# Moving a statistics visit and 98 adds between engines in a hybrid decoder kernel whose order a planner writes

## The chip, the cores and the metric

The kernel runs on one core of a Trainium2 chip. The metric is the device time of one execution in microseconds. An order of instructions is fixed for each of five queues: TensorE (PE), VectorE (DVE), ScalarE (ACT), GpSimd (POOL), and SyncE (SP), which here issues all DMAs.

## The reference

One decoder layer over 4096 tokens of width 1024, in float32: a root-mean-square norm, one input projection, two groups of heads that read it, a gate on each, one output projection, a residual add and a final norm.

```
h = rmsnorm(x, norm_w);  u = h @ w_in
GLA, 4 heads:   S_t = diag(a_t) S_{t-1} + k_t^T v_t;  o_t = q_t S_t    (in chunks)
                o = o * rsqrt(mean(o^2) + eps) * gla_norm_w;  gla_out = o * silu(gg)
RWKV, 8 heads:  mixed = cols + (prev - cols) * mu;  r, rk, rv, wl, al = split(mixed)
                kk = rk * k_k / |rk * k_k|        (norm over the head's 64 columns)
                k  = rk * (1 + (a - 1) * k_a)
                S_t = S_{t-1} (diag(w_t) - kk_t^T (a_t kk_t)) + v_t^T k_t;  y_t = S_t r_t
                y  = group_norm(y) * ln_w + ln_b
                bonus = sum(r * k * r_k over the head) * v
                rwkv_out = (y + bonus) * silu(rg)
out = rmsnorm(x + concat(gla_out, rwkv_out) @ w_out, final_norm_w)
```

## The kernel before, in words

Activations are held with the features on the partitions and 512 tokens along the free dimension: 8 blocks of 512 tokens. In each block the RWKV group is worked off in 4 units of two heads (128 partitions), 32 units in all, and the GLA group in 2 pairs. Every large projection is made of fp16 parts: 8 matmuls for each of three products of high and low halves, 24 of 128x128 by 128x512. The weights are split into these halves in the first block, from raw tiles that SP loads 512 KB at a time, and stored to DRAM, from where later blocks load them again.

A sum over the features of a head, or of all partitions, is a *statistics visit* (`stat_mm`, L816): four float32 matmuls with a 128x32 matrix of ones and zeros, each writing 32 rows of one PSUM bank, so the array works as four tiles of 128x32. The profile shows each float32 matmul as two, so a visit is eight. In `rwkv_ab` (L961) a unit has two: the key norm (`stat_mm(pst, bones, rn)`, L995), whose result goes through a reciprocal root (`newton`) and over DRAM to all partitions (`bcast`, one store and two broadcasting loads), and, near the unit's end, the bonus sum (L1063), which is copied by ScalarE, spread in the same way and multiplied by v on VectorE. `rwkv_d` (L1183) has the third, of the output norm, and adds the bonus to it. `bones` has ones in column 0 for the first head and in column 16 for the second, so two of every 32 result rows are used.

The squares of the input (`x_block`, L867) and of the output (`out_block`, L1382) are summed over 8 feature tiles before one visit: ScalarE squares a tile, GpSimd adds it. GpSimd also runs most units' 62-step triangular inversion on small tiles.

The program text does not fix the order. Eight streams (input blocks, weights, the RWKV chain, its inverse, GLA, the two projections and the output) generate steps with their dependences. A planner then runs a list schedule forwards and backwards over all steps with costs of its own (`cost`, `forward`, `backward`), 24 rounds of it (`ROUNDS`; a nonzero seed adds random noise to the ranks), keeps the best by its own clock, and gives tiles of one kind their buffers by it (`settle`). The instructions are issued in that order. Tiles of one kind share buffers, so the names in the profile are those of the buffer that a tile was given, not of the variable in the text. All engine calls go through one line (L533), so rows are told apart by tile and shape.

Of the kernel before, what the change touches and what calls it, by code (L numbers as in the profile page):

```python
# [20 lines left out]
P = 128  # L21
# [21 lines left out]
EL = 0.0  # L43
PB = {"ch": 1}
NBK = 7
ROUNDS = ((0, 0.0, 1.083, 2.0, 5.0), (0, 0.0, 0.7, 2.0, 5.0), (0, 0.0, 0.7, 2.0, 5.0), (0, 0.0, 0.7, 2.0, 5.0),
# [5 lines left out]
KINDS = ((True, "dt.float32", 512), (False, "dt.float32", 512), (False, "dt.float16", 1024), (False, "dt.float16", 2048), (False, "dt.float32", 1024), (False, "dt.float32", 128))  # L52
OWN = ("EP", "x16")
NC = TB // C
# [34 lines left out]
def hymba_kernel(ctx, tc, xT, wt, wg, wo, wua, gup, pk, ck, out):  # L89
# [163 lines left out]
    def put(t0, eng, d, lag, cols, tiles, tab, port, outs, ins, f):  # L253

        keys = lambda aps: {k: k in {y for x in aps for y in leased(x)} for a in aps for k in whole(a)}
        ki, ko = keys(ins), keys(outs)
        for k in list(ki) + list(ko):
            t0 = max(t0, wkey.get(k, 0.0))
        for k in ko:
            t0 = max(t0, rkey.get(k, 0.0))  # L260
        s = Step(len(steps), t0, eng, d, lag, cols, tiles, tab, port, f)
        for k in {**ki, **ko}:
            if isinstance(k[0], int):
                leases[k[0]].setdefault(k[1:], []).append(s)
        got = lambda m: m.lag - 0.1 * (m.eng == eng and eng in "VSG")
        for k, timed in ki.items():
            rkey[k] = max(rkey.get(k, 0.0), t0)
            if k in wlast:
                s.follow(wlast[k], got(wlast[k]) if timed else None)
        for k, timed in ko.items():  # L270
            wkey[k] = t0
            if k in wlast:
                s.follow(wlast[k], got(wlast[k]) if timed and eng != "T" and not (eng == wlast[k].eng == "D" and k[0] in stores) else None)
            for m in readers.get(k, ()):
                s.follow(m, (0.95 if m.eng == "D" else 0.1) if timed else None)
            wlast[k], readers[k] = s, []
        for k in ki:
            if k not in ko:
                readers.setdefault(k, []).append(s)
        if eng == "T":  # L280

            if last[0] and last[1] == turn[0] and last[0].form == s.form != (4, 4):
                last[0].next = s
                s.follow(last[0], None)
            last[:] = [s, turn[0]]
        for m in s.on:
            m.to.append(s)
        steps.append(s)
# [9 lines left out]
    def forward(rank, ahead=0.0, bonus=2.0):  # L298


        wait, can, free = {e: [] for e in "VSGTD"}, {e: [] for e in "VSGTD"}, dict.fromkeys("VSGTD", 0.0)
        pes, tab, run, port, ends = Array(), 0, None, 0.0, {"V": 0.0, "G": 0.0}
        left, ready, start = [len(x) for x in befores], [0.0] * len(steps), [0.0] * len(steps)
        end, push, pop = [0.0] * len(steps), heapq.heappush, heapq.heappop
# [3 lines left out]
        for _ in steps:  # L308
            t = 1e18
            for x in "VSGTD":  # L310
                if can[x]:
                    y = free[x]
                elif wait[x]:
                    y = max(free[x], wait[x][0][0])
                else:
                    continue
                if y < t:
                    t, e = y, x
            if t == 1e18:
                return None, None  # L320
            w, c = wait[e], can[e]
            while w and w[0][0] <= t:
                n = pop(w)[1]
                push(c, (rank[n], n))
            if e == "T":
                x = next((x for x in c if run and x[1] == run.n), None)
                x = x or min(heapq.nsmallest(12, c), key=lambda x: x[0] - bonus * (steps[x[1]].form == pes.form))
                run = steps[x[1]].next
                c.remove(x)
                heapq.heapify(c)  # L330
            else:
                x = pop(c)
                if e in "VS":
                    soon = [y for y in heapq.nsmallest(4, w) if y[0] < t + ahead * steps[x[1]].d and rank[y[1]] < x[0] - (y[0] - t)]
                    if soon:
                        y = min(soon, key=lambda y: rank[y[1]])
                        push(c, x)
                        w.remove(y)
                        heapq.heapify(w)
                        x = (rank[y[1]], y[1])  # L340
            n = x[1]
            s = steps[n]
            t, d = max(t, ready[n]), s.d
            if e == "T":
                t, d = pes.put(t, d, s.cols, s.tiles)
                free["T"], z = pes.free, t + d
            elif e == "D":
                free["D"], port = t + 0.45, max(t + 1.28, port) + d
                z = port
            else:  # L350
                if s.tab is not None:
                    d, tab = d + 1.2 * (s.tab != tab), s.tab
                if s.port:
                    d += max(0.0, ends["G" if e == "V" else "V"] - (0.1 if e == "V" else 0.05) - t)
                    ends[e] = t + d
                free[e] = z = t + d
            start[n], end[n] = t, z
            for m, lat in nexts[n]:
                y = t if lat is None else z + lat
                if y > ready[m]:  # L360
                    ready[m] = y
                left[m] -= 1
                if not left[m]:
                    push(wait[steps[m].eng], (ready[m], m))
# [42 lines left out]
    def cost(eng, op, ins, n, o):  # L407
# [10 lines left out]
            runs = 0.13 if n == 64 and psum else 0.09 if len(o.shape) > 2 and o.shape[-1] == 64 and n == 512 else 0.0  # L418
            return (0.075 if n < 256 else 0.11) + 0.05 * (fast and n > 16) + 0.04 * (few > 0 and n > 16) + n / (1920 if fast else 960) + runs
        if eng == "G":  # L420
            return 0.155 + 0.07 * few + n * (2.0 if len(big) > 1 else 0.4 if not ins else 0.95) / 960
        return (0.125 if n == 64 and o.shape[0] == 64 else 0.11 if n > 64 and o.shape[0] < 128 and psum else 0.0) + (0.052 if psum else 0.094) + n / 1200 + 0.09 * (few > 0)

    def shares(op, aps, n):
# [179 lines left out]
    D.dma_start(pkt, pk)  # L604
    mc = sb(one, [P, 4, P], U8, "mc")
    mg = sb(one, [P, 4, P], U8, "mg")
    bones = sb(one, [P, 32], F32, "bones")
    c64 = sb(one, [P, 64], F32, "c64")
    smask = sb(one, [P, TB], U8, "smask")
    gmask = sb(one, [P, TB], U8, "gmask")  # L610
# [206 lines left out]
        for g in range(4):  # L817
            T.matmul(ps[32 * g:32 * g + 32, 0:P], lhsT=ones, rhs=src[:, P * g:P * g + P], start=first, stop=last)

    def bcast(rows, heads, o, st):  # L820

        d = sb(dr, [heads, 4, P], F32, "bcd" + st, 8)
        if heads == 2:
            D.dma_start(d.rearrange("h g t -> g h t"), rows[0:P:16])
        else:
            D.dma_start(d[0], rows[0:P:32])
        n = P // heads
        for h in range(heads):
            D.dma_start(o[n * h:n * h + n], d[h:h + 1].rearrange("h g t -> h (g t)").broadcast_to((n, TB)))
# [37 lines left out]
    def x_block(b):  # L867
# [3 lines left out]
        for k in range(KT):  # L871
# [8 lines left out]
                S.activation(acc, x, AF.Square)  # L880
            else:
                S.activation(xr, x, AF.Square)
                G.tensor_tensor(acc, acc, xr, ALU.add)
        if b == 0:
            yield from norm_weight()
        else:
# [71 lines left out]

    lo, hi = slice(0, 64), slice(64, 128)

    def rwkv_ab(u, p, b, xs, LR):  # L961
        W = Wt[u % NBUF].rearrange("p c (a t) -> p c a t", a=7)
        nb = Wt[u % NBUF][:, :, 192:320]
# [28 lines left out]
        yield after(rn)  # L992

        pst = yield from need("r")
        stat_mm(pst, bones, rn)  # L995
        bcast(newton(pst[:, 0:P], None, None, 1e-24, "a"), 2, rn, "a")
        V.scalar_tensor_tensor(rn, rk, pkt[:, PK_KK + p:PK_KK + p + 1], rn, ALU.mult, ALU.mult)
        V.scalar_tensor_tensor(ta, ta, 1.0, rn, ALU.add, ALU.mult)
# [59 lines left out]
        S.activation(tg, pg, AF.Tanh, scale=hinv[:, i:i + 1])  # L1058
        V.scalar_tensor_tensor(tg, tg, 1.0, pg, ALU.add, ALU.mult)
        rel("r")  # L1060
        yield after(r)
        pst = yield from need("r")
        stat_mm(pst, bones, r)  # L1063
        brow = sb(rt, [P, P], F32, "nya")
        S.copy(brow, pst[:, 0:P])
        bv = tA("bv", 2)
        bcast(brow, 2, bv, "b")
        V.tensor_tensor(bv, bv, v, ALU.mult)
        rel("r")
        pt = yield from need("r", 2)  # L1070
        for c in range(NC):
            T.transpose(f4(pt[c // 4])[:, c % 4, :], bk[:, c, :], ident)
# [54 lines left out]
    def rwkv_c(u, p, b, mgt, st_):  # L1127
# [43 lines left out]
        for c in range(NC):  # L1171
            for q_, e in dd:
                T.matmul(py[q_, c, :], lhsT=sv[:, c, e, :], rhs=W[:, c, 5 + e, :], start=False, stop=c == NC - 1)
        yield lambda: done["C"] == done["CC"]
        y = sb(rt, [P, TB], F32, "cy")
        rs = sb(rt, [P, TB], F32, "crs")
        S.copy(y, py.rearrange("p c t -> p (c t)"))
# [204 lines left out]
    def out_block(b, mgt):  # L1382
# [7 lines left out]
        for n in range(KT):  # L1390
# [9 lines left out]
                S.activation(acc, mgt[n], AF.Square)  # L1400
            else:
                S.activation(xr, mgt[n], AF.Square)
                G.tensor_tensor(acc, acc, xr, ALU.add)
        yield after(acc)
        pst = yield from need("o")
        stat_mm(pst, gones, acc)
# [70 lines left out]
            D.dma_start(out[P * n:P * n + P, TB * b:TB * b + TB], part[n])  # L1477
        yield now[0]

    done = dict.fromkeys(("A", "C", "G", "GE", "GV", "GG", "GH", "I", "CC", "O", "X", "W", "SU", "N", "V"), 0)  # L1480


    def norm_weight():
# [229 lines left out]
```

## Time and profile before

| | |
|---|---|
| three runs | 2224.54, 2225.80, 2226.07 us, median 2225.80 |
| profiled execution | 2224.65 us, span of its instructions 2222.8 us |
| PE busy | 2162.6 us (97%), 20190 matmuls, mean granted clock 0.993 |
| DVE busy | 1669.9 us (75%) |
| ACT busy | 1308.1 us (59%) |
| POOL busy | 865.4 us (39%) |
| DMA | 325.06 MB, 48.4% of 16 engines on SP's queue |

Busy time of PE counts pipelined matmuls, whose ends overlap; the intervals between starts tell what each one holds the array for. A row in the timeline merges like instructions that follow each other: its time is from the first start to the last end.

### The profile page before, as it was taken

What the parts mean: (1) busy time and instruction counts of PE and PEld (TensorE: products, weight loads), DVE (VectorE), ACT (ScalarE), POOL (GpSimd) and SP (SyncE); (2) the same over time, 40 slices, a digit from 0 to 9 for tenths busy, and PEclk for the clock granted to TensorE, in tenths of its full rate; (3) what the DMA queues carried; (4) which work ended last, traced back from release to release, by engine and by line L of the source; (5) the groups of instructions that cost most, each with busy time, mean ns of one, the idle gap of its engine ahead of it and who ended that gap; (6) DMA issues with size and microseconds to landing.
All of it is one profiled execution on the core that took longest, in us unless ns stands there. A gap on an engine that the chain in (4) does not pass through costs nothing.

```text
span 2222.8 us, 53967 instructions
## 1 busy us (share of the span) xinstructions
PE 2162.6 (97%) x20190; PEld 1326.6 (60%) x20190; DVE 1669.9 (75%) x3679; ACT 1308.1 (59%) x3678; POOL 865.4 (39%) x2209
## 2 busy tenths in 40 slices
PE   5999999999999999999999999999999999999997
PEld 2656666456755667557574566655666565655654
DVE  6888889849777586857877677776878658786786
ACT  6766776545765566555664556645566554655463
POOL 4243444552246431454416344265125543054400
PEclk9999999999999999999999999999999999999999
DMA  9577455545345453445534463354634545444342
GB/s 298 159 243 239 147 162 170 167 110 177 110 136 157 127 168 113 141 138 160 151 97 148 127 186 112 94 152 142 191 93 140 151 122 168 114 117 116 109 124 72
DMA packets 274220, 325.06 MB, mean 146 GB/s; under 512 B 129652, under 2 KB 131876, under 8 KB 273956
## 3 DMA queue, kind: packets, MB, share of 16 engines
q1 hardware_dynamic: 273956, 321.60, 48.4%
q8 instruction: 158, 2.59, 0.5%
q14 instruction: 106, 0.87, 0.1%
HBM read 276.45 MB, written 45.05 MB: 145 GB/s over the span
## 4 chain that ended last, share of the span: by engine, by line
PE 83%; DVE 8%; DMA 3%; ACT 2%; issue 1%; SPq 1%; DVEq 0%; ACTq 0%
PE bank L533 72%; PE ch L533 11%; DVE W L533 1%; SPq L533 1%; DVE x L533 1%; DMA wdr<-wo 1%; DMA wg<-wdr 0%; DVE mgr L533 0%; DVE gt L533 0%; DVE wo L533 0%; DVE vt L533 0%; DMA x<-in_wt_dram 0%; DVE SC L533 0%; ACT wo L533 0%; DVE Ta L533 0%
## 5 line engine op out<-in xcount | busy, mean ns | idle before, releaser
L533 PE MATMUL bank<-x,wr 128*128 128x512 f16 x2392 | 619.5, 381 | 1.8 <-DMA wr<-wdr 1.3
L533 PE MATMUL bank<-x,wg 128*128 128x512 f16 x1736 | 452.7, 381 | 2.8 <-ACT sv L533 1.6
L533 PEld LDWEIGHTS <-wr 128*128 128x128 f16 x2832 | 274.4, 100 | 257.6 <-issue 12.8
L533 POOL TENSOR_TENSOR Tc<-Tc,tm 128x60 f32<-128x60 f32 (+24 forms) x961 | 353.4, 368 | 73.0
L533 PE MATMUL bank<-x,wo 128*128 128x512 f16 x1326 | 320.6, 380 | 0.0
L533 PEld LDWEIGHTS <-wg 128*128 128x128 f16 x1968 | 190.5, 100 | 178.8 <-issue 10.8
L533 POOL TENSOR_TENSOR tm<-Tc,bk 128x60 f32<-128x60 f32 (+24 forms) x403 | 147.7, 367 | 376.4 <-DMA bk<-nd 266.7
L533 PEld LDWEIGHTS <-wo 128*128 128x128 f16 x1488 | 145.3, 100 | 137.4 <-issue 1.9
L533 POOL TENSOR_TENSOR tm<-Tc,sv 128x60 f32<-128x60 f32 (+24 forms) x310 | 114.4, 369 | 274.3 <-DMA sv<-nd 106.5
L533 PEld LDWEIGHTS <-x 128*128 128x128 f16 x3096 | 195.6, 99 | 29.6 <-issue 5.3
L533 DVE COPY_PREDICATED W<-mc,bank 64x512 f32<-64x512 uint8 x228 | 162.1, 724 | 15.3 <-PE bank L533 10.2
L533 ACT COPY us<-bank 64x64 f32<-64x64 f32 x432 | 89.1, 206 | 63.1 <-PE bank L533 56.5
L533 PE MATMUL ch<-x,wr 128*128 128x512 f16 x440 | 114.0, 381 | 0.0
L533 PE MATMUL bank<-wg,x 128*128 128x128 f16 x1376 | 108.3, 219 | 0.8 <-DMA wg<-wdr 0.8
L533 PE MATMUL bank<-wr,x 128*128 128x128 f16 x1216 | 96.5, 219 | 0.1
L533 ACT ACTIVATE sa<-bank,mu_s 128x512 f32<-128x512 f32 x91 | 62.4, 686 | 57.1 <-PE bank L533 55.8
L533 PEld LDWEIGHTS bank<-us,W 128*128 128x128 f32 x432 | 75.2, 191 | 28.5 <-ACT us L533 5.2
L533 ACT ACTIVATE psd<-rk,PC 128x64 f32<-128x64 f32 x256 | 88.7, 346 | 5.7
L533 DVE SCALAR_TENSOR_TENSOR bk<-bank,PC,psd 64x64 f32<-64x64 f32 x140 | 39.5, 282 | 67.8 <-PE bank L533 65.0
L533 DVE SCALAR_TENSOR_TENSOR sv<-bank,PC,psd 64x64 f32<-64x64 f32 x154 | 43.5, 282 | 58.4 <-PE bank L533 55.3
L533 PE MATMUL bank<-us,W 128*128 128x64 f32 x432 | 78.8, 264 | 2.3 <-ACT us L533 1.7
L533 ACT COPY sv<-bank 64x64 f32<-64x64 f32 (+2 forms) x216 | 59.4, 275 | 35.4 <-PE bank L533 30.8
(2347 smaller groups left out, 4471.7 us busy)
## 6 DMA issues: line engine op xcount, KB each, us to landing
wr<-wdr SPq DMA_DIRECT2D x253, 256.0 KB
wg<-wdr SPq DMA_DIRECT2D x185, 256.0 KB
wo<-wdr SPq DMA_DIRECT2D x128, 256.0 KB
x<-in_wt_dram SPq DMA_DIRECT2D x29, 512.0 KB
wdr<-wo SPq DMA_DIRECT2D x24, 512.0 KB
mgg<-in_xT_dram SPq DMA_DIRECT2D x32, 256.0 KB
bk<-nd SPq DMA_DIRECT2D x52, 128.0 KB
sv<-nd SPq DMA_DIRECT2D x40, 128.0 KB
```

The costliest lines, as they stand in the source:

```text
L533: put(t0, self.name, d, lag, cols, tiles, tab, port, outs, ins, lambda: f(*[moved(x, ids) for x in a], **{k: moved(x, ids) for k, x in kw. ...
```

## The change

The bonus sum of a unit is no longer a visit of its own. `bones` becomes a slice of a 40-column tile whose first 8 columns are zero, and `bonus` is the same tile shifted by 8 columns, so that the bonus sums fall in the 8th and 24th row of each 32. The next unit's key norm visit runs `stat_mm` twice into one bank, first on its own squares, then with `bonus` on the last unit's product of r and k; the copy, the spread and the product with v follow there (`bonus_rows`). The very last unit keeps its own visit. The output norm's step waits until its bonus is done. The 98 adds of squares are issued on VectorE. Several of the planner's figures change: the delay between dependent instructions of one engine, the time at which each engine starts, the time of a memset on GpSimd, and a limit on how far DMA issue runs ahead of the transfers. `ROUNDS` has 26 entries, 20 of them with a seed, in place of 24 with 14.

```
-ROUNDS = ((0, 0.0, 1.083, 2.0, 5.0), ...   (24 rounds)
+ROUNDS = ((0, 0.0, 1.149, 2.0, 5.0), ...   (26 rounds)
...
-        got = lambda m: m.lag - 0.1 * (m.eng == eng and eng in "VSG")
+        got = lambda m: {"V": 0.11, "S": 0.08, "G": 0.03}.get(eng, m.lag) if m.eng == eng else m.lag
...
-        ... = ..., dict.fromkeys("VSGTD", 0.0)
+        ... = ..., {"V": 0.8, "S": 2.0, "G": 0.8, "T": 0.0, "D": 0.75}
...
-                free["D"], port = t + 0.45, max(t + 1.28, port) + d
-                z = port
+                z = port = max(t + 1.28, port) + d
+                free["D"] = max(t + 0.45, port - 2.0)
...
-            return 0.155 + 0.07 * few + n * (2.0 if len(big) > 1 else 0.4 if not ins else 0.95) / 960
+            return 0.05 + n / 1200 if not ins else 0.155 + 0.07 * few + n * (2.0 if len(big) > 1 else 0.95) / 960
...
-    bones = sb(one, [P, 32], F32, "bones")
+    bones2 = sb(one, [P, 40], F32, "bones")
+    G.memset(bones2[:, 0:8], 0.0)
+    bones, bonus = bones2[:, 8:40], bones2[:, 0:32]
...
-    def bcast(rows, heads, o, st):
+    def bcast(rows, heads, o, st, n0=0):
...
-            D.dma_start(d.rearrange("h g t -> g h t"), rows[0:P:16])
+            D.dma_start(d.rearrange("h g t -> g h t"), rows[n0:P:16])
...
-                G.tensor_tensor(acc, acc, xr, ALU.add)      (in x_block and in out_block)
+                V.tensor_tensor(acc, acc, xr, ALU.add)
...
+    def bonus_rows(u, pst, n):
+        bv, v = bvs.pop(u)
+        brow = sb(rt, [P, P], F32, "nyc")
+        S.copy(brow, pst[:, 0:P])
+        bcast(brow, 2, bv, "b", n)
+        V.tensor_tensor(bv, bv, v, ALU.mult)
+        done["B"] += 1
...
-        stat_mm(pst, bones, rn)
+        stat_mm(pst, bones, rn, True, u == 0)
+        if u > 0:
+            r = last_r.pop()
+            stat_mm(pst, bonus, r, False, True)
+            bonus_rows(u - 1, pst, 8)
...
-        yield after(r)
-        pst = yield from need("r")
-        stat_mm(pst, bones, r)
-        brow = sb(rt, [P, P], F32, "nya")
-        S.copy(brow, pst[:, 0:P])
         bv = tA("bv", 2)
-        bcast(brow, 2, bv, "b")
-        V.tensor_tensor(bv, bv, v, ALU.mult)
-        rel("r")
+        bvs[u] = bv, v
+        if u == 4 * NB - 1:
+            yield after(r)
+            pst = yield from need("r")
+            stat_mm(pst, bones, r)
+            bonus_rows(u, pst, 0)
+            rel("r")
+        else:
+            last_r.append(r)
...
-        yield lambda: done["C"] == done["CC"]
+        yield lambda: done["C"] == done["CC"] and done["B"] > u
```

## Rows read from the trace of the kernel before

**Rows 1.** Stretches: us; busy PE, PEld, DVE, ACT, POOL (count); clock, DMA share, GB/s.

```profile
0.00:60.00 60.00, 35.48 (x190) 17.45 (x190) 39.03 (x102) 40.50 (x78) 22.42 (x41) 0.97 0.89 292
60.00:110.00 50.00, 48.89 (x452) 32.08 (x451) 41.55 (x92) 34.69 (x64) 15.44 (x41) 1.00 0.50 155
110.00:300.00 190.00, 183.71 (x1768) 115.88 (x1767) 159.61 (x364) 133.62 (x335) 67.18 (x161) 0.96 0.66 206
300.00:2100.00 1800.00, 1789.28 (x16793) 1096.22 (x16792) 1338.40 (x2873) 1042.53 (x3026) 760.36 (x1967) 1.00 0.47 138
2100.00:2150.00 50.00, 45.48 (x495) 30.12 (x493) 47.36 (x157) 31.13 (x95) 0.00 (x0) 0.97 0.32 96
2150.00:2222.80 72.80, 59.74 (x503) 34.81 (x501) 43.94 (x97) 25.63 (x84) 0.00 (x0) 0.93 0.31 99
```

**Rows 2.** Timeline of PE around unit 0's bonus visit: start, us, instruction, tiles, count.

```profile
117.99 1.03 PE L533 MATMUL bank<-x,wg 128*128 128x512 f16 x4
118.95 0.43 PE L533 MATMUL bank<-go,bones 128*32 128x128 f32 x8
119.31 0.60 PE L533 MATMUL bank<-x,wg 128*128 128x512 f16 x2
```

**Rows 3.** Timeline of PE at two visits in a row.

```profile
919.05 0.42 PE L533 MATMUL bank<-xacc,gtwo 128*32 128x128 f32 x8
919.29 0.40 PE L533 MATMUL bank<-mgg,gtwo 128*32 128x128 f32 x8
919.62 0.82 PE L533 MATMUL bank<-x,wr 128*128 128x512 f16 x3
```

**Rows 4.** Timeline of PE: unit 30's bonus visit; unit 16's bonus beside another visit.

```profile
2076.62 0.43 PE L533 MATMUL bank<-mgg,bones 128*32 128x128 f32 x8
...
1159.89 0.42 PE L533 MATMUL bank<-xr,bones 128*32 128x128 f32 x8
1160.13 0.40 PE L533 MATMUL bank<-bv,bones 128*32 128x128 f32 x8
```

**Rows 5.** Timeline of SP: stores of bonus 27, key norm 28, output norm 27.

```profile
1886.89 0.57 SPq L533 DMA_DIRECT2D bcdb<-gt  x1
...
1917.45 0.57 SPq L533 DMA_DIRECT2D bcda<-nyg  x1
...
1968.89 0.57 SPq L533 DMA_DIRECT2D bcdc<-gt  x1
```

**Rows 6.** Instructions of one tile: adds on each engine, ns min/median/max, first, last start.

```profile
L533 POOL TENSOR_TENSOR xacc<-xacc,mgr x3: 1267/1267/1667, 2014.0 to 2070.4; 128x512 f32<-128x512 f32 x3
...
L533 DVE TENSOR_TENSOR mgg<-mgg,xr x2: 669/674/679, 781.3 to 2090.7; 128x512 f32<-128x512 f32 x2
```

**Rows 7.** Timeline of DVE near 28 us.

```profile
28.14 1.77 DVE L533 TENSOR_TENSOR x<-mgg,x 128x512 f16<-128x512 f32 x1
```

**Rows 8.** Timeline of POOL near 28 us.

```profile
28.11 1.26 POOL L533 TENSOR_TENSOR gg<-gg,v 128x512 f32<-128x512 f32 x1
```

**Rows 9.** The page's costliest groups: POOL's inversion; busy us, mean ns, idle before.

```profile
L533 POOL TENSOR_TENSOR Tc<-Tc,tm 128x60 f32<-128x60 f32 (+24 forms) x961 | 353.4, 368 | 73.0
```

**Rows 10.** Timeline of SP from 39 to 50 us.

```profile
39.62 0.33 SPq L533 DMA_DIRECT2D r<-in_wo_dram  x1
...
46.02 1.30 SPq L533 DMA_DIRECT2D E<-in_gup_dram  x2
47.41 0.37 SPq L533 DMA_DIRECT2D x<-in_wt_dram  x1
...
49.33 1.28 SPq L533 DMA_DIRECT2D x<-in_wt_dram  x1
```

**Rows 11.** The chain that ended last, near 50 us: start, us, what.

```profile
49.33 6.90 DMA x<-in_wt_dram
```

**Rows 12.** Timeline of ACT near 50 us, idle before it in brackets.

```profile
50.34 0.42 ACT L533 ACTIVATE SC<-E 128x256 f32<-128x256 f32 x1 [5.22 <-DMA E<-in_gup_dram]
```

**Rows 13.** Timeline of PE near 30 us, idle before it in brackets.

```profile
30.49 0.79 PE L533 MATMUL ch<-ident,amW 128*128 128x128 f32 x2 [8.37 <-ACT wo L533]
```

More of the change, by code (lines that the diff above doesn't have):

```diff
@@ L45 @@
 NBK = 7
-ROUNDS = ((0, 0.0, 1.083, 2.0, 5.0), (0, 0.0, 0.7, 2.0, 5.0), (0, 0.0, 0.7, 2.0, 5.0), (0, 0.0, 0.7, 2.0, 5.0),
[5 rows of a table removed]
+ROUNDS = ((0, 0.0, 1.149, 2.0, 5.0), (0, 0.0, 0.7, 2.0, 5.0), (0, 0.0, 0.7, 2.0, 5.0), (0, 0.0, 0.7, 2.0, 5.0),
[6 rows of a table added]
 KINDS = ((True, "dt.float32", 512), (False, "dt.float32", 512), (False, "dt.float16", 1024), (False, "dt.float16", 2048), (False, "dt.float32", 1024), (False, "dt.float32", 128))
@@ L298, in forward @@
     def forward(rank, ahead=0.0, bonus=2.0):
-        wait, can, free = {e: [] for e in "VSGTD"}, {e: [] for e in "VSGTD"}, dict.fromkeys("VSGTD", 0.0)
+        wait, can, free = {e: [] for e in "VSGTD"}, {e: [] for e in "VSGTD"}, {"V": 0.8, "S": 2.0, "G": 0.8, "T": 0.0, "D": 0.75}
         pes, tab, run, port, ends = Array(), 0, None, 0.0, {"V": 0.0, "G": 0.0}
@@ L882, in x_block @@
                 S.activation(xr, x, AF.Square)
-                G.tensor_tensor(acc, acc, xr, ALU.add)
+                V.tensor_tensor(acc, acc, xr, ALU.add)
         if b == 0:
@@ L959, in hymba_kernel @@
     lo, hi = slice(0, 64), slice(64, 128)
+    last_r, bvs = [], {}
+    def bonus_rows(u, pst, n):
[5 more added lines that the diff above has]
+        done["B"] += 1
     def rwkv_ab(u, p, b, xs, LR):
@@ L1402, in out_block @@
                 S.activation(xr, mgt[n], AF.Square)
-                G.tensor_tensor(acc, acc, xr, ALU.add)
+                V.tensor_tensor(acc, acc, xr, ALU.add)
         yield after(acc)
@@ L1478, in out_last @@
         yield now[0]
-    done = dict.fromkeys(("A", "C", "G", "GE", "GV", "GG", "GH", "I", "CC", "O", "X", "W", "SU", "N", "V"), 0)
+    done = dict.fromkeys(("A", "C", "G", "GE", "GV", "GG", "GH", "I", "CC", "O", "X", "W", "SU", "N", "V", "B"), 0)
     def norm_weight():
```

11 rows, old and new, of the table ROUNDS are left out of this document.

## The prediction

> **What bounds the kernel now.** First the busy times by stretch [rows 1], to see where TensorE still has idle time. From 300 to 2100 us it is busy for 1789.28 of 1800 us at full granted clock: 10.7 us of idle in four fifths of the run. The rest of its idle lies at the ends: 24.5 us before 60, 1.1 from 60 to 110, 6.3 from 110 to 300, 4.5 from 2100 to 2150, 13.1 after. VectorE has 1338.40 us of work in the same 1800 (74%), GpSimd 760.36 (42%). So in the middle only TensorE's own time counts: what it does, and what it loses when it changes between the full array and small tiles. A wait on another engine counts at the two ends, or if it grows past what TensorE's other streams fill.
>
> Then TensorE's timeline around one statistics visit, which is the unit of the main edit [rows 2]. A fp16 matmul of 512 columns follows its like every 0.215 us (four span 1.03 us and two 0.60: (1.03 - 0.60) / 2). The four in the first row so begin at 117.99, 118.20, 118.42 and 118.64, a fifth would begin at 118.85, and the visit begins at 118.95: 0.10 us late. The next full matmul begins 0.36 us after the visit. A visit on its own therefore costs 0.45 us. Two visits in a row [rows 3] take 919.62 - 919.05 = 0.57 us, so the second costs 0.21 us and no change of form. Joining a lone visit to another is worth 0.45 - 0.21 = 0.24 us where both neighbours are full-array work.
>
> **The change part by part.**
>
> *The bonus sums.* Each of 32 units has a key norm visit, a bonus visit and an output norm visit. The edit takes 31 bonus visits (all but the last unit's) and appends them to the following unit's key norm, accumulating in the same bank; the 8th and the 24th result row of each 32 carry the new sums. The matmuls stay the same in number. Not all 31 gain: the planner joins visits already where it can. Following each bonus copy on ScalarE back to its visit I find 20 of the 31 alone (the first in [rows 2], the last of them the first row of [rows 4]); the other 11 stand next to another visit, as 1159.89 and 1160.13 do in [rows 4], and they gain nothing by being joined. Of the 20, 12 have full matmuls on both sides: 12 x 0.24 = 2.9 us. Seven have a group of another small form as a neighbour, where a change of form is paid anyway: I take 0.45 - 0.10 - 0.21 = 0.14 each, 1.0 us. One stands beside a group of its own form and gains nothing. Together 3.9 us. The bounds: 0, if the planner loses as many other joints as it gains, and 31 x 0.24 = 7.4, if the joined visits join with others as often as the lone ones did.
>
> The rest of the step moves with it: one ScalarE copy of 128x128, one store and two reading DMAs on SP, one VectorE product per unit. On SP these three (the store takes 0.57 us of SP in [rows 5]) now come beside the key norm's own three and can put its spread back by about 1.7 us. That norm feeds the unit's scores, and TensorE's cover for it is the projections of the other streams: in the middle it waits 10.7 us in all. I cost it at nothing; with that cover gone it would be 31 x 1.7 = 53 us, which only a tenfold growth of TensorE's waits could show, so I don't let it widen the range. The new wait at the key norm, on the previous unit's product of r and k, holds back the in-order queue of TensorE, but that product is made before the previous unit's scores. The new wait behind it is the output norm, which adds the bonus. In unit 27, the one with the least room, the bonus store is issued at 1886.89, the next key norm's at 1917.45, the output norm's at 1968.89 [rows 5]: 51 us still separate the new place from the user. Over the 31 units the next key norm comes between 13 us before and 53 us after the present bonus, so r and v live some 8 us longer on average and bv begins later. One bank lease per unit goes. Nothing late follows from this.
>
> *The sums of squares.* 7 adds for each of 7 input blocks and 7 output blocks, 98 of 128x512. On GpSimd one takes 1.27 us, on VectorE a sum of two such tiles 0.67 [rows 6]. GpSimd loses 124 us, VectorE gains 66 (74% becomes about 78% in the middle). The chain that ends in the block's statistic gets shorter by 0.6 us per add; it is not on the path. What VectorE delays lies in the same 10.7 us of waits: I take 0. The ends are -1 (a tenth of that idle) and +9.4, worked out below as a rival.
>
> The two engines are not free of each other: at 28.14 a VectorE subtraction took 1.77 us beside a GpSimd add from 28.11 to 29.37 [rows 7, 8], where 29.37 - 28.14 + 0.67 makes 1.90, so it nearly had to wait the other out. The long holds of 1.27 us go with this change; what is left on GpSimd is mostly the inversion's small ops. The Trainium skill says in "SBUF — State Buffer", section "Who interferes with whom", that a VectorE instruction with both inputs in SBUF and a GpSimd one that reads SBUF block each other for the whole instruction; that speaks against the change, since all 98 new VectorE adds are of this kind. The trace agrees that one waits the other out, with the 1.77 us. By the rule each new add could wait for one small op more, 0.37 us on the mean [rows 9]; 98 of them are 36 us of VectorE time, which the middle would hide, and the 14 of the VectorE rival below would cost 5.2 us more, 2236.5 in place of 2231.3.
>
> *Figures of the beginning and the rounds.* These change the order only. The one that can matter is the DMA figure: the planner now holds an issue back until the queue has 2 us of work left. In the trace SP issues eight 256 KB loads of output weights from 39.62 us on, needed last of all weights, and behind them the two raw input weights at 47.41 and 49.33 [rows 10]. The last one is on the chain of waits for 6.90 us [rows 11]. 512 KB at the 292 GB/s of the first 60 us [rows 1] are 1.8 us; with 2 us ahead it lands after about 3.8 plus some overhead, so I take 2.5 us less. ScalarE also waits 5.22 us for a small load issued at 46.02 behind the same ones [rows 10, 12]. Bounds: +3 (the start is a different order too, and may be a worse one) and -8 (nearly the 8.37 us for which TensorE waits before 30.49 for one weight's scale [rows 13]). The new rounds: no row prices them; I take 0, with 3 us either way, from a middle whose whole idle is 10.7 us.
>
> *Sum.* -3.9 - 2.5 + 0 + 0 = -6.4. The profiled execution took 2224.65 (span 2222.80 and 1.85 around it), so 2218.25; the median of the three runs is 1.15 above that execution, so 2219.4.
>
> **The rivals.**
>
> *The order eats the gain.* The visits are joined, but other joints between visits are lost, as the key norm now brings a fixed pair, and the start stays as it is. For: 11 of 31 bonus visits are joined today with no help. Against: TensorE's own work cannot grow by it. Time: 2225.8 + 0 to - 3, about 2224.5.
>
> *VectorE becomes the limit at the ends (slower).* Place: the stretch from 2100 to 2150, where VectorE is busy 47.36 of 50 us and TensorE idles 4.5 [rows 1], and the beginning, where VectorE has 41.55 of 50 from 60 to 110. If the 7 adds of the last ordinary output block fall in the one and the 7 of the second input block in the other, each costs its 0.67: 14 x 0.67 = 9.4 us, less 3.9 for the visits: 2231.3. It decides from the point where these adds are placed after 2100, or after 55 us. Against it: today the output adds are done by about 2071 [rows 6] and the second input block's are under way at 28 us [rows 8].
>
> *The beginning gives much more.* The idle before 60 us is 24.5, most of it behind weights that arrive late, and from 110 to 300 the granted clock is 0.96 [rows 1], a mean of stretches at 2.4 and at 1.2 GHz, which is 7.6 us of full-speed time lost. If the better order of loads takes a third of the idle, 8 us, with the visits' 3.9: 2225.8 - 11.9 = 2213.9.
>
> **How the numbers follow.** My forecast 0.45 (own range 2215 to 2223.5), the beginning 0.20, the order eats it 0.22, VectorE at the ends 0.13. The range from 2209 to 2230 takes in the forecast, the larger start gain with part of its bounds, and the no-change case with its 3 us; most of the slower rival is left out. A change below 0.2% (4.45 us) can't be told from none here. Faster by more, below 2221.35: three quarters of the forecast, all of the beginning, little of the others, 0.57. Slower by more, above 2230.25: 0.13 with most of the VectorE rival and a little of the order. Within: 0.30.
>
> **What would show it.** In the profile after: the bonus sums as a second group of eight small matmuls right behind a key norm's, 0.57 us for both; fewer changes of form on TensorE between 300 and 2100, with its busy time down by 3 to 5 us; GpSimd's busy time down by about 124 us and VectorE's up by 66; TensorE's idle before 110 us below 25.6, and output weight loads after the raw input weights in SP's queue. The forecast is wrong if TensorE's idle from 300 to 2100 grows beyond 15 us, if the idle after 2100 passes 20, or if the start's idle rises.

## The result, and the profile after

The changed kernel takes 2188.62 us (median of four runs, 2186.92 to 2189.49) against 2225.94 for the kernel before on the same chip: a ratio of 0.984, 95% interval 0.9824 to 0.9856. It is faster by 37 us where 6.4 were forecast, and lies 20 us below the range.

The first part of the page after, engines' busy times:

```profile
PE 2145.3 (98%) x20190; PEld 1324.4 (61%) x20190; DVE 1692.5 (77%) x3777; ACT 1314.4 (60%) x3678; POOL 752.8 (34%) x2112
```

The stretches of the kernel after, with the columns of [rows 1] (us; busy PE, PEld, DVE, ACT, POOL with counts; granted clock; DMA share; GB/s):

```profile
0.00:60.00 60.00, 41.52 (x242) 20.71 (x243) 44.03 (x126) 46.96 (x90) 12.80 (x35) 0.97 0.83 272
60.00:110.00 50.00, 48.24 (x439) 31.78 (x437) 44.78 (x96) 35.89 (x62) 15.38 (x35) 1.00 0.80 263
110.00:300.00 190.00, 188.23 (x1852) 122.57 (x1851) 164.33 (x393) 146.17 (x381) 94.33 (x229) 1.00 0.64 200
300.00:2100.00 1800.00, 1793.76 (x17037) 1106.52 (x17036) 1380.16 (x3033) 1046.11 (x3020) 630.25 (x1815) 1.00 0.48 138
2100.00:2150.00 50.00, 47.27 (x446) 29.06 (x444) 33.49 (x79) 32.15 (x114) 0.00 (x0) 1.00 0.43 125
2150.00:2187.70 37.70, 26.28 (x182) 13.74 (x182) 25.71 (x54) 7.13 (x13) 0.00 (x0) 0.86 0.15 57
```

The span fell by 35.1 us (2222.8 to 2187.7). TensorE's busy time fell by 17.3 and its idle time by 17.8 (60.2 to 42.4). By stretch, against [rows 1]: idle before 110 us 25.6 to 20.2, from 110 to 300 6.3 to 1.8, from 300 to 2100 10.7 to 6.2, after that 17.6 to 14.2. So 9.9 of the 17.8 went before 300 us. Windows of equal time do not hold equal work, so these four numbers say where idle vanished, not which step did it.

The busy time has three parts. One is the clock. From 110 to 300 us the granted clock rises from 0.96 in [rows 1] to 1.00. In the kernel before, these three windows hold it down in the profiled execution (same columns):

```profile
144.80:148.20 3.40, 3.40 (x11) 1.66 (x10) 2.84 (x9) 2.87 (x5) 0.00 (x0) 0.50 0.43 145
206.30:209.70 3.40, 3.40 (x10) 1.21 (x8) 3.22 (x9) 2.15 (x3) 0.00 (x0) 0.50 0.83 236
216.50:223.30 6.80, 6.80 (x34) 4.80 (x33) 4.68 (x11) 2.86 (x9) 0.00 (x0) 0.50 0.49 136
```

TensorE's timeline of the kernel before, just ahead of the last of them (idle before the instruction in brackets):

```profile
215.65 0.60 PE L533 MATMUL bank<-W,bk 64*128 64x128 f32 x6 [2.01 <-ACT W L533]
```

A wait of 2.01 us for a ScalarE result is followed by 6.8 us at 0.50, which is 1.2 GHz. The 13.6 us of the three windows did 6.8 us of full-speed work. After the change, this stretch has no such window. Half of all time at 0.50 between the first and the last matmul, worked out from the clock's records in the two traces, is 10.6 us before and 2.5 after: 8.1 of the 17.3 us. That is one execution of each. Over all executions of the kernel before, the mean granted clock goes from 0.991 to 0.997 (mean 0.9944 of 83), over the four of the kernel after from 0.996 to 0.998 (0.997); by these means the clock is worth about 6 us.

The second part is the joined visits. In TensorE's records of the two traces, sorted by start, the stretches of work in 128x32 tiles fall from 115 to 96: 19 entries into this form fewer, at 0.24 us each 4.6 us. Some 5 us are left without a name.

### The profile page after: what moved, and what is told of

It reads as the page before. It is cut to its first block, busy times and chain, and to the rows that moved or that the text cites. A ratio compares the mean times of both kernels' runs of the same rounds, so it can differ in the third digit from the quotient of the medians.

```text
span 2187.7 us, 53996 instructions
## 1 busy us (share of the span) xinstructions
PE 2145.3 (98%) x20190; PEld 1324.4 (61%) x20190; DVE 1692.5 (77%) x3777; ACT 1314.4 (60%) x3678; POOL 752.8 (34%) x2112
## 4 chain that ended last, share of the span: by engine, by line
PE 86%; DMA 4%; DVE 4%; ACT 2%; issue 1%; SPq 0%; DVEq 0%; ACTq 0%
PE bank L534 76%; PE ch L534 10%; DMA wdr<-wo 1%; DMA wg<-wdr 1%; DMA x<-in_wt_dram 0%; DVE mgg L534 0%; DVE W L534 0%; DMA wr<-wdr 0%; ACT wo L534 0%; SPq L534 0%; DMA wo<-wdr 0%; DMA bcdc<-nyg 0%; ACT L534 0%; DMA vt<-nd 0%; ACT x L534 0%
## 5 line engine op out<-in xcount | busy, mean ns | idle before, releaser
L534 PE MATMUL bank<-x,wr 128*128 128x512 f16 x2392 | 640.4, 380 | 4.4 <-ACT wr L534 3.3
L534 PE MATMUL bank<-x,wg 128*128 128x512 f16 x1880 | 505.1, 379 | 2.0 <-DMA wg<-wdr 1.6
L534 POOL TENSOR_TENSOR tm<-Tc,sv 128x60 f32<-128x60 f32 (+24 forms) x372 | 139.3, 374 | 307.6 <-DMA sv<-nd 195.6
L534 POOL TENSOR_TENSOR tm<-Tc,bk 128x60 f32<-128x60 f32 (+24 forms) x310 | 105.5, 340 | 394.8 <-DMA bk<-nd 331.9
L534 PE MATMUL bank<-wr,x 128*128 128x128 f16 x1536 | 128.2, 219 | 0.0
L534 POOL TENSOR_TENSOR tm<-Tc,vt 128x60 f32<-128x60 f32 (+24 forms) x155 | 58.3, 376 | 179.7 <-DMA vt<-nd 70.7
L534 POOL TENSOR_TENSOR tm<-Tc,f 128x60 f32<-128x60 f32 (+24 forms) x124 | 45.7, 368 | 142.8 <-DMA f<-nd 108.1
L534 POOL MEMSET Tc<- 32x8 f32 (+1 forms) x160 | 24.5, 153 | 202.9 <-DMA td<-Tc 197.6
L534 ACT ACTIVATE psd<-rn,PC 128x64 f32<-128x64 f32 x256 | 88.8, 347 | 6.8 <-DVE Sst L534 0.4
L534 ACT COPY sv<-bank 64x64 f32<-64x64 f32 (+2 forms) x212 | 56.9, 270 | 42.4 <-PE bank L534 39.0
L534 PE MATMUL ch<-x,wr 128*128 128x512 f16 x288 | 78.3, 379 | 0.0
```

What stands on the lines that cost most here:

```text
L534: put(t0, self.name, d, lag, cols, tiles, tab, port, outs, ins, lambda: f(*[moved(x, ids) for x in a], **{k: moved(x, ids) for k, x in kw. ...
```

## The experiments

Every ratio is to the kernel before on the same chip, in brackets its 95% interval. A difference between two kernels is that of their ratios, times 2225.9, where no medians are named. The planner makes a new order for any edit it sees, so the first three runs fix the order and change only what is issued.

**The adds in an order made for GpSimd.** s2_adds_vector: the order of the kernel before, the 98 adds planned as GpSimd work but issued on VectorE.

```diff
+    GV = Engine("G", nc.vector)
...
-                G.tensor_tensor(acc, acc, xr, ALU.add)
+                GV.tensor_tensor(acc, acc, xr, ALU.add)      (in x_block and in out_block)
```

> The kernel before in its own order with only the 98 adds issued on VectorE. If the adds on GpSimd held the old order up, 2225.9 falls by 5 us or more. If they were hidden, within 3 us. If VectorE is the limit at the ends (the slower rival), it rises by up to 9 us.

1.0011 (0.9997 to 1.0025), 2225.67 us: no difference. Moving the adds to VectorE is worth nothing to an order that was made for GpSimd.

**The adds in an order made for VectorE.** s1_adds_gpsimd: the order of the kernel after, the adds issued on GpSimd.

```diff
+    VG = Engine("V", nc.gpsimd)
...
-                V.tensor_tensor(acc, acc, xr, ALU.add)
+                VG.tensor_tensor(acc, acc, xr, ALU.add)      (in x_block and in out_block)
```

> The changed kernel in its own order, instruction for instruction, with only the 98 adds of squares issued on GpSimd in the places that the plan gave them on VectorE. If the adds matter by what they cost on an engine (the long holds of 1.27 us on GpSimd, the queueing of its inversion behind them), the time rises by 5 to 20 us from 2188.6, with more idle time of TensorE. If TensorE's cover hides it, as the prediction had it, it stays within 3 us.

0.9947 (0.993 to 0.9964), 2210.89 us: 22 us slower than the kernel after by the medians, just above the 5 to 20 expected. The middle of s1_adds_gpsimd (columns as above):

```profile
300.00:2100.00 1800.00, 1782.67 (x16830) 1094.63 (x16828) 1317.73 (x2880) 1036.59 (x2994) 725.50 (x1909) 1.00 0.47 137
```

TensorE's waits from 300 to 2090 us in s1_adds_gpsimd (us in total, times, longest):

```profile
PE bank L534 <- DVE vt L534: 4.1, 4, 2.6
PE bank L534 <- DVE nya L534: 3.4, 1, 3.4
PE bank L534 <- DVE bk L534: 3.2, 4, 1.5
```

Its middle idles for 17.3 us where the kernel after idles for 6.2, and the longest waits are for VectorE. One of them, on the timelines of TensorE, VectorE and GpSimd:

```profile
947.41 0.58 PE L534 MATMUL bank<-vt,W 128*128 128x128 f32 x1 [2.62 <-DVE vt L534]
945.90 0.82 DVE L534 TENSOR_TENSOR mgr<-v,bv 128x512 f32<-128x512 f32 x1 [5.28 <-POOL qi L534]
944.61 1.26 POOL L534 TENSOR_TENSOR qi<-qi,mgr 128x512 f32<-128x512 f32 x1
```

VectorE idled 5.28 us for one of the moved adds, which reads the tile that VectorE writes next, and TensorE idled 2.62 us for what VectorE does behind it. The order counts on a GpSimd free of the adds; not every wait was followed back like this one. This run by itself does not say that the edit is worth 22 us: f101_bonus_figures, below, plans the adds on GpSimd and loses little.

**The joined visit.** s3_parted: the order of the kernel after, but in 27 of the 31 joined visits the second group is moved behind one full-array matmul.

```diff
+            joined.append(steps[-4:])
...
+        for four in joined:
+            at = max(order.index(s) for s in four)
+            i = next(i for i in range(at + 1, len(order)) if order[i].eng == "T" and order[i].form == (4, 4))
...
+                order = [s for s in order[:i + 1] if s not in four] + four + order[i + 1:]
...
```

> The changed kernel in its own order, but in 27 of the 31 joined visits one full matmul that follows in TensorE's order is put between the key norm's eight matmuls and the bonus's eight. If a joined visit saves the two changes of form (0.24 us each), this costs 27 x 0.24 = 6.5 us: about 2195. If the joining is worth nothing by itself and the gain is all in the order, within 2 us of 2188.6.

0.9873 (0.9854 to 0.9892), 2195.47 us: 6.9 slower than the kernel after by the medians. TensorE's timeline of the kernel after at one joined visit:

```profile
338.00 0.38 PE L534 MATMUL bank<-x,wg 128*128 128x512 f16 x1
338.31 0.43 PE L534 MATMUL ch<-mgr,bones 128*32 128x128 f32 x8
338.55 0.40 PE L534 MATMUL ch<-gep,bones 128*32 128x128 f32 x8
338.89 0.39 PE L534 MATMUL bank<-x,wr 128*128 128x512 f16 x1
```

The same place in s3_parted:

```profile
338.58 0.38 PE L535 MATMUL bank<-x,wg 128*128 128x512 f16 x1
338.89 0.43 PE L535 MATMUL ch<-mgr,bones 128*32 128x128 f32 x8
339.25 0.39 PE L535 MATMUL bank<-x,wr 128*128 128x512 f16 x1
339.57 0.43 PE L535 MATMUL ch<-gep,bones 128*32 128x128 f32 x8
339.92 0.49 PE L535 MATMUL bank<-vt,sv 128*128 128x128 f32 x2
```

From the full matmul ahead to the work behind both groups it is 0.89 us joined (338.00 to 338.89) and 1.34 us parted (338.58 to 339.92). 0.21 of that is the matmul put between, so joining is worth 0.24 us, the 0.45 - 0.21 of [rows 2, 3]; 27 of them are 6.5. TensorE's busy time says the same: 2152.1 us parted, 2145.3 joined, with the clock's loss alike (2.6 and 2.5), and 123 stretches of 128x32 work in place of 96. This prices joining in the order of the kernel after. Against the kernel before only 19 of these stretches are gained, as its planner had joined visits without the edit: 4.6 us.

**Each edit with an order of its own.** The next five kernels take the edits in combinations. All plan with unseeded rounds, the best of four walks by the planner's own clock, so that none is favoured by a list of seeds found for it. In the line below `first` and `rest` stand for each kernel's own numbers (0.7 to 1.149, and 4 to 16 in all kernels so planned). f000_before_plain has no edit, f100_bonus the joined sums, f010_adds the adds, f001_figures the planner's figures, f111_all_plain all three.

```diff
+ROUNDS = ((0, 0.0, first, 2.0, 5.0),) + ((0, 0.0, 0.7, 2.0, 5.0),) * rest
```

> The kernel before with nothing changed but the list of rounds: no noise in any of them, and the walk cut off where the planner's own clock was best (of four such walks of 24 rounds). If the listed rounds of the changed kernel are a matter of a longer search, an order found with so little search is slower than the listed one before, by 5 to 15 us: 2231 to 2241. If any order is about as good, 2221 to 2231.

1.0026 (1.0016 to 1.0035), 2229.62 us: the listed rounds of the kernel before are worth 6 us to it, no more than the luck of an order measured below.

> The kernel before with the bonus sums joined to the next key norm as its only edit, planned afresh with rounds without noise (the best of four walks of 24, as for the kernel at 2229.6). If joining saves only the visits, 4 to 8 us below that: 2222 to 2226. If it also gives the order room, 15 us or more below: 2215 or less.

0.996 (0.9946 to 0.9974), 2214.99 us, just at the 2215 named for an order that also gains room; its second order, below, does not repeat that.

> The kernel before with the adds on VectorE as its only edit, planned afresh in the same way. If the adds on GpSimd cost the order, which can now be made for VectorE, 5 to 15 us below 2229.6; if they are hidden, within 4 us of it.

1.0015 (1.0 to 1.0029), 2227.74 us.

> The kernel before with the planner's four figures as its only edit, planned afresh in the same way. If the figures of the beginning make the unexpected gain, TensorE's idle before 300 us falls from 33 by 8 us or more and the time to 2220 or less. If they give what the prediction took, 2.5 us: about 2227.

0.9991 (0.9975 to 1.0007), 2220.03 us. The time is at the bound named, but TensorE's idle before 300 us is 29.2, so it did not fall by the 8 us that were named with it.

> The changed kernel with all its edits, but planned by rounds without noise as the others here: 2188.6 if the listed rounds are worth nothing, 2195 to 2205 if the longer search made a part of the gain.

0.9898 (0.9874 to 0.9922), 2201.98 us. This is where it was to be if the listed rounds made a part of the gain: 13 us of it. Against f000_before_plain the edits alone give 15, 2 and 8 us, all three together 28. That is a sum within a few us; whether the adds are needed in it, and how much of each term is the luck of one order, was open.

**Two edits, adds left on GpSimd.** f101_bonus_figures: joined sums and figures.

> The bonus sums joined and the planner's figures, the adds left on GpSimd and planned there, rounds without noise (best of four walks). Beside the kernel with all three edits so planned (2202, ratio 0.990) it prices the adds where the order is made for them: at 22 us if they cost what they do when put on GpSimd in an order made for VectorE, at 0 to 5 if a fresh order hides them.

0.9871 (0.9853 to 0.9888), 2193.3 us. The adds are not needed: with them (f111_all_plain) the time is no lower. Against f000_before_plain this is 34 us, 12 more than the 15 and 8 of the two edits alone.

**Is it the order's own luck?** h_100b, h_101b and h_001b repeat joined sums alone, joined sums with figures, and figures alone by another walk, so in a second order.

> Bonus sums joined as the only edit, in a second order from another walk without noise. 2210 to 2220 if the first one's 2215 is what this edit gives; within 6 us of 2193 if that was a bad order and the figures are worth nothing.

0.9999 (0.9983 to 1.0015), 2220.73 us.

> Bonus sums joined and all four figures in a second order from another walk without noise. Within 6 us of the first one's 2193 (ratio to before 0.984 to 0.990) if the figures and not the luck of one order make the step; 2205 or more if that order was lucky.

0.9898 (0.9875 to 0.9922), 2203.51 us: the ratio is in the range named, the time nearly at the 2205 named for luck.

> The planner's figures as the only edit in a second order. Near the first one's 0.999 of before if the figures need the joined sums to be of use; 0.990 or less if the first order was a bad one and the two edits simply add up (figures 20 us, joined sums 7).

0.9981 (0.9971 to 0.9991), 2221.0 us. Two orders of one program differ by 9, 6 and 2 us. The means of the pairs are 0.998 for the joined sums, 0.9986 for the figures and 0.9885 for both; against f000_before_plain that is 10, 9 and 31 us, again 12 more than the sum. With up to 9 us between two orders of one program, and one order of f000_before_plain, the times do not make this certain.

**Which figure.** From f101_bonus_figures one figure at a time is set back: h_nogot the delay between dependent instructions of one engine, h_noport the limit on how far DMA issue runs ahead, h_nostart the start times and the memset.

```diff
 h_noport
-                z = port = max(t + 1.28, port) + d
-                free["D"] = max(t + 0.45, port - 2.0)
+                free["D"], port = t + 0.45, max(t + 1.28, port) + d
+                z = port
```

> Bonus sums joined and the planner's figures (2193.3 with all four, 2215 with none), but without the one for the delay between dependent instructions of one engine, planned afresh in the same way. If that figure makes the orders agree better with the chip (VectorE's dependent 128x128 instructions follow each other every 0.33 us, by the old figure every 0.24), the time goes back to 2205 or more. If it is another figure, it stays below 2200.

0.9928 (0.9902 to 0.9954), 2207.75 us.

> As h_nogot, but without the limit on how far DMA issue runs ahead instead. If the limit makes the gain, as the prediction had it for the beginning, 2205 or more with TensorE's idle before 300 us back above 24; if not, below 2200.

0.9936 (0.9911 to 0.9961), 2209.9 us.

> As h_nogot, but without the start times of the engines and the memset's figure instead. These touch the first few us alone; I expect 2190 to 2199. 2205 or more if the beginning hangs on them.

0.99 (0.9875 to 0.9925), 2201.75 us. Against the mean with all figures the losses are 9.7, 11.5 and 3.5 us. By the times named beforehand, 2205 or more, both the delay and the DMA limit count. But each is one order, and the interval of h_101b, which has all figures, reaches those of h_nogot and h_noport, so these two losses are hardly larger than the luck of an order. For the DMA limit the stretches speak as well. h_noport:

```profile
0.00:110.00 110.00, 85.52 (x624) 47.25 (x626) 79.67 (x195) 73.42 (x137) 39.67 (x95) 0.95 0.69 223
110.00:300.00 190.00, 181.83 (x1785) 117.84 (x1784) 160.47 (x364) 140.10 (x347) 67.99 (x172) 0.98 0.67 213
```

and f101_bonus_figures, which has the limit:

```profile
0.00:110.00 110.00, 90.94 (x679) 51.88 (x680) 92.03 (x214) 83.09 (x151) 46.81 (x95) 1.00 0.77 260
110.00:300.00 190.00, 186.52 (x1864) 122.27 (x1863) 161.73 (x386) 147.38 (x386) 83.57 (x216) 1.00 0.65 201
```

TensorE's idle before 300 us is 32.7 without the limit, above the 24 named, and 22.5 with it (22.7 in h_101b). Over all orders that were planned afresh, the idle before 110 us is 15.6 to 20.6 us in the ten with the limit (mean 18.3) and 22.6 to 25.6 in six of the seven without it (f010_adds has 19.1; mean 23.3). So the limit takes some 5 us of idle off the beginning.

**Rounds.** The listed rounds could be a longer search that would have helped the kernel before just as much. n_before2, n_after1 and n_after2 replace them by another list: in each round the best of 25 candidates (seed, noise, ahead, bonus) by the planner's clock, 27 rounds for the program before, 9 and 33 for the one after.

> The kernel before with another list of rounds from the same search, 27 rounds, within 4 us of the listed order by the planner's clock. If orders of one program that look alike to the planner differ little on the chip, 2222 to 2230; if luck counts for 10 us, anything from 2215 to 2240.

1.0002 (0.9992 to 1.0013), 2224.32 us.

> The changed kernel with another list of rounds, 9 of them, found by a fresh search (in each round the best of 25 candidates by the planner's own clock). By the planner's clock its order is as good as the listed one or 6 us better. If the listed order of the changed kernel is one like others, 2183 to 2192; if it was a lucky one on the chip, nearer to the 2202 of the order planned without noise.

0.9868 (0.9852 to 0.9885), 2193.35 us, 1 us outside the range.

> As n_after1 with another search, 33 rounds. 2183 to 2192 if the listed order is one like others, 2195 or more if it was lucky.

0.9824 (0.9809 to 0.9839), 2182.92 us. The same search brings the old program to where it was and the changed one to 2183, so the listed order of the kernel after was not a lucky one, and a longer search alone does not make the gain. It makes a part of it: over unseeded rounds such lists win 7, 13 and 16 us for the changed program and 5 and 6 for the old one. n_after2 is the fastest kernel measured; its interval overlaps that of the kernel after, so it is faster than the kernel before, and than the kernel after only by its median. Its stretches:

```profile
0.00:110.00 110.00, 94.41 (x702) 54.75 (x703) 93.17 (x226) 88.55 (x162) 31.04 (x77) 1.00 0.84 275
110.00:300.00 190.00, 186.76 (x1834) 121.31 (x1833) 161.36 (x390) 141.62 (x377) 92.02 (x223) 1.00 0.63 200
300.00:2100.00 1800.00, 1794.04 (x17063) 1108.34 (x17062) 1381.61 (x3046) 1046.53 (x3031) 631.07 (x1814) 1.00 0.47 139
2100.00:2180.80 80.80, 66.64 (x596) 38.40 (x594) 52.91 (x118) 34.15 (x110) 0.00 (x0) 0.95 0.29 92
```

It idles 15.6 us before 110, against 20.2 in the kernel after, with the clock at 1.00 from the start.

**The runs side by side.** Span and TensorE's busy time from each page, idle their difference (us of the one profiled execution; that of n_after1 was 8 us slower than its other three):

| edits | kernels | PE busy | PE idle |
|---|---|---|---|
| none | before, f000_before_plain, n_before2 | 2162.6, 2162.5, 2162.5 | 60.2, 63.3, 62.2 |
| adds | s2_adds_vector, f010_adds | 2161.1, 2163.8 | 60.7, 63.3 |
| figures | f001_figures, h_001b | 2159.4, 2159.2 | 62.2, 61.1 |
| joined sums | f100_bonus, h_100b | 2152.6, 2152.8 | 64.7, 64.9 |
| joined sums, figures | f101_bonus_figures, h_101b | 2143.7, 2152.0 | 45.8, 52.6 |
| all | f111_all_plain, n_after1, after, n_after2 | 2144.8, 2143.3, 2145.3, 2141.8 | 55.5, 56.7, 42.4, 39.0 |

The row to see in each page is its first; of f100_bonus:

```profile
PE 2152.6 (97%) x20190; PEld 1328.3 (60%) x20190; DVE 1671.0 (75%) x3679; ACT 1324.0 (60%) x3678; POOL 852.1 (38%) x2210
```

and of f101_bonus_figures:

```profile
PE 2143.7 (98%) x20190; PEld 1326.9 (61%) x20190; DVE 1674.6 (76%) x3679; ACT 1322.3 (60%) x3678; POOL 860.6 (39%) x2210
```

The joined sums alone take 10 us off the busy time and nothing off the idle. A part of the 10 is clock: half the time at 0.50 in which TensorE was busy is 9.5 to 10.5 us in the first row, 4.9 and 8.4 in these two. The figures alone take 3 off the busy time and nothing off the idle. Idle below 60 us appears in the six orders with both edits, and in none of the nine without. It also appears in h_nogot, h_noport and h_nostart (52.1, 57.2 and 50.7), so no one figure is needed for it. The nearest two rows are 56.7 and 60.2, and each is one execution. In the middle, from 300 to 2100 us, the idle of the freshly planned orders goes from 6.0 to 19.3 us, and no edit decides it: 6.0 to 17.7 with both, 8.8 and 17.9 with the joined sums, 16.6 and 17.0 with the figures, 9.9 to 17.0 with neither. The two orders with figures alone also idle less before 110 us (17.9 and 18.9) and lose it again in the middle.

## Why the prediction was wrong

The direction held, and so did the visits. The step that failed is the last of the change's parts, "figures of the beginning and the rounds", costed at -2.5 and 0. Along one path through the runs, from f000_before_plain, the joined sums give 10 us (mean of two orders), the figures behind them 21 (mean of two), the adds -3, the listed rounds 13, and the 6 that the old list was worth go off: 36 us. Figures and rounds are so 28 of it, where 2.5 were forecast with bounds of +6 and -11. Each of these steps carries the luck of its orders, 2 to 9 us, and with the figures put first they give 9 and the joined sums 23.

- *"The one that can matter is the DMA figure", costed at -2.5 with bounds of +3 and -8.* The mechanism is there. SP's timeline after the change:

```profile
35.88 0.44 SPq L534 DMA_DIRECT2D x<-in_wt_dram  x1
...
39.55 0.33 SPq L534 DMA_DIRECT2D x<-in_wt_dram  x1
...
40.94 0.43 SPq L534 DMA_DIRECT2D r<-in_wo_dram  x1
41.42 2.30 SPq L534 DMA_DIRECT2D mgg<-in_wo_dram  x4
```

  The raw input weights now go ahead of the output weights, which stood in front of them in [rows 10], and the idle before 110 us falls by 5.4, as it does in the other orders with the limit (5.0 by the means). I priced one late weight; h_noport has 10 us more idle before 300 us and loses 11.5. The other figures I put at nothing with no row for it. h_nogot, which has the DMA limit, loses 9.7, near the luck of an order.
- *The rounds: "I take 0, with 3 us either way, from a middle whose whole idle is 10.7 us".* The width was mis-sized. What an order can win is not the middle's idle alone, but all of TensorE's idle (60.2 us) and what the clock loses (10.6). Of the measured 35.1 us of span, 17.8 are idle and 8.1 are clock, where the forecast had 2.5 for the start and the rounds together. [Rows 1] show the idle of every stretch and a clock of 0.96; I added up one stretch. Net of the 6 us that the old list was worth, the listed rounds gave 7.
- *The rival "the beginning gives much more"* named the right two sources, the idle before weights and the clock of 0.96, and priced 8 us. The stretch to 300 us gave 9.9 of idle (31.9 to 22.0) and 6.8 of clock (7.6 in the prediction, from the rounded 0.96), near half of the 35.1.
- *Visits, -3.9, with bounds of 0 and -7.4.* This term held. The price of one, 0.24 us, is what s3_parted measures, and the 19 stretches of 128x32 work that vanish against the kernel before make 4.6 us. The 11 visits that I took as no gain were joined before, and the rival in which the order eats the gain did not come. The Trainium skill says in "TensorEngine Tiling (Array Packing)", section "Key Properties", that a change of tiling mode drains the engine; the trace agrees, with 0.45 us for a group that is entered and left and 0.21 for one more in the same mode.
- *Adds, 0.* s2_adds_vector and f010_adds agree. The rival in which VectorE becomes the limit at the ends did not come: from 2065 to 2115 us, as far from the end of the shorter run, VectorE is busy for 43.57 of 50 us where it had 47.36 [rows 1], and TensorE idles 0.95 us in place of 4.5.
- *The 66 us more on VectorE* were wrong: GpSimd's busy time fell by 112.6 (forecast 124), and VectorE's rose by 22.6. In s2_adds_vector, where nothing else changes, GpSimd loses 125 us and VectorE gains 24.2 (31.0 in the summed times of its instructions, whose ends overlap). As 98 x 0.67 = 66, its other instructions became about 35 us shorter. One that waited for an add is that of [rows 7, 8]. The same instruction in s2_adds_vector, on VectorE's timeline:

```profile
28.10 0.82 DVE L533 TENSOR_TENSOR x<-mgg,x 128x512 f16<-128x512 f32 x1
```

  1.77 us has become 0.82. The Trainium skill's rule in "SBUF — State Buffer", section "Who interferes with whom", that such a pair of instructions block each other whole, fits that row, and here it has the opposite sign to the one I drew from it: fewer long holds outweigh more short ones. None of it reached the time of s2_adds_vector (1.0011).

What stays open is whether the figures need the joined sums at all. The times give both together 12 us more than each alone, but that is near the luck of these orders, and it lies in the middle's idle and in the clock, which differ as much between orders of one program. Shown is that with unseeded rounds the adds are not needed (no listed order without them was measured), that a longer search alone is not the reason, that joining is worth 0.24 us a visit, and that the DMA limit takes some 5 us of idle off the beginning. TensorE's waits from 110 to 2100 us in f001_figures and f100_bonus are spread over many tiles, the longest 3.8 us.

## What to carry to other kernels

Where a planner writes the order, price an edit of its cost figures by all the idle of the bounding engine and the time it ran at a low clock, not by the idle of the longest stretch; a term that no row can price deserves a width taken from that, on both sides. Measure an edit both in the old order and in an order of its own: the adds cost 0 in one order, 22 us in another, and gain 0 where the planner may choose. One order says little below the difference between two orders of the same program, here 2 to 10 us; make a second before believing such a gain.

## What was not expected of the hardware

- A short wait can be followed by a longer loss: behind the 2.01 us at 215.65 come 6.8 us at a granted 0.50. In the two profiled executions the clock gave back 8.1 us, near half as much as the idle time itself.
- Without 98 GpSimd adds of 1.27 us beside it, VectorE's other work took about 35 us less, so moving 66 us of work onto VectorE made it only 24 busier (s2_adds_vector).
